# A decoder step's first tiles: order of first loads, rule for weight stores, staging buffers, single-token attention and the end of each attention

## The chip, the cores and the metric

The kernel runs on the 8 cores of one Trainium2 chip, as one program whose cores don't talk to each other. The metric is the device time of the slowest core in microseconds (us). Most executions agree within 0.3%; in some, the cores of one die run at a lower clock and the time is some per cent longer. Those slow runs are left out of every comparison here. Experiments ran on several chips, each beside the kernel before, so kernels of different calls are compared by their ratio to the kernel before.

## The reference, cut to what matters

One layer of a decoder, on 16 prompts of 2048 tokens and 32 single tokens with a cache:

```python
x = x + 0.5 * swiglu(rmsnorm(x, g1), w_gate1, w_up1, w_down1)      # FFN1, 1024 -> 2816 -> 1024
z = rmsnorm(x, g_mix) @ w_in       # pooling input | 3 head groups of q,k,v | gate_pool | gate_attn
# ... branch A: trailing means over 2, 4, 8, 16 tokens, a linear map for each group, -> w_pool_br
# ... branch B: window attention, (window, dilation) = (128,1), (512,4), (2048,16), rotary q and k,
#     the three outputs merged by their softmax denominators, -> w_attn_br
x = x + (sigmoid(gate_pool) * A + sigmoid(gate_attn) * B) @ w_o
x = x + 0.5 * swiglu(rmsnorm(x, g2), w_gate2, w_up2, w_down2)      # FFN2
# ... final rmsnorm; the rotated keys and the values are outputs too, in float32
```

All weights are float32 in memory; the kernel multiplies in bfloat16.

## The kernel before

Each core has 2 prompts and 4 single tokens (the "sample" rows). A prompt is 4 tiles of 512 tokens, so tiles 0 to 7. For each tile the program goes through a projection (q, k, v), an attention and a gate part, and fills TensorE's order there with matmuls of an FFN: FFN1's last third in tile 0, FFN2 of the tile before in the others. FFN1 of tiles 0 and 1 comes first and shares its weights. The single tokens ride along in the first tiles.

Weights stream in tiles of 512 KB bfloat16. The first use of a tile loads the float32 original, converted on the way, from GpSimd's queue (`w<-wt`). One of the uses then writes the bfloat16 copy to a scratch in memory (`wscr<-w`), and later uses load that copy from the Sync engine's queue (`w<-wscr`). `store_at` says which use writes it; until then each use is a float32 load.

```python
def store_at(tid):
    late = tid[0][:2] in ("gp", "ga", "wo") or tid[0] in ("wg1", "wu1", "wd1")
    return 1 if late and tid[1] % 2 else 0          # 0: first use stores, 1: second use
# ... w_issue: nth is how often this tile was loaded before
if nth <= at:
    pool.dma(slot[:, :], wt_d[ti, :, :], wsem[s][0], writes=slot.r)                    # float32, converted
else:
    sp.dma(slot[:, :], wscr[ti, :, :], wsem[s][2], reads=[scr_res[ti]], writes=slot.r) # bfloat16 copy
# ... wget, at the use itself
if first:
    sp.dma(wscr[ti, :, :], wsl[s][:, :], wsem[s][1], reads=wsl[s].r, writes=[scr_res[ti]])
```

In the projection a block of 128 tokens goes through small staging buffers, two each of `vst` (values), `kf` and `vf` (float32 keys and values), whose store is issued at once:

```python
sp.dma(v2scr[H.h, b * 128:(b + 1) * 128, :], vs[:, :], ds_vs.next(), reads=vs.r, writes=[v2res[H.h]])
v = vf.next()
dve.op(lambda: nc.vector.tensor_copy(out=v[:, :], in_=ps[bk][:, 256:512]), reads=[psr[bk]], writes=v.r)
sp.dma(kvp_d[2][s, r0:r0 + 128, 1, :], v[:, :], ds_vf.next(), reads=v.r)
# ... keys
rope_add(a_, b_, c0, c0 + 256, k_[:, :], k_.r)
sp.dma(dst, k_[:, :], ds_kf.next(), reads=k_.r)
```

The attention keeps up to three scored steps waiting for their product with V. At its end all three are consumed in one piece (`drain`), and `finish` scales the sums to `attnT`, which the gate part reads:

```python
def drain():
    while live:
        consume()      # two groups of PV matmuls, then perhaps a merge of `tot` on VectorE
    finish()
thunks.append(drain)
```

`K.later(t, f)` puts f off in the program's order by t us of TensorE work; `K.need(tag)` forces what was put off.

The softmax here doesn't subtract the row's maximum and nothing guards it: scores larger than these inputs give would overflow.

## Time and profile before

The median was 2959.34 us in the first four runs. The prediction shows the page's head, the stretches and the waits of the bad ones. More of TensorE's table of waits over the whole span of the kernel before (total us, times, longest us):

```profile
PE ps L590 <- DVE h L584: 36.8, 11, 22.7
...
PE ps L272 <- DVE tot L1248: 23.4, 26, 5.3
PE ps L272 <- DVE x L875: 13.2, 9, 2.8
```

`h` is the normalised block that TensorE transposes; its longest wait is the start of the kernel. `tot` are the merges of the attention: 26 waits for 23.4 us, spread over all tiles. In one quiet tile, the attention of tile 3 (1326 to 1412 us), they look like this:

```profile
PE ps L272 <- DVE tot L1248: 2.3, 4, 1.3
PE ps L272 <- DVE x L875: 1.1, 1, 1.1
```

VectorE updates `x` only after the merges.

### The profile page before, as it was taken

To read this page: it belongs to the slowest core of one execution; us is meant where nothing else is said; L and a number is where in the kernel's file an instruction comes from. 1 tells how busy PE (TensorE), PEld (TensorE's weight loads), DVE (VectorE), ACT (ScalarE), POOL (GpSimd) and SP (SyncE) were. 2 spreads that over 40 slices of the span, in tenths; PEclk is the share of its full clock that TensorE was granted. 3 is DMA by queue.
4 is the path that set the end of the run, shared out by engine and by line. 5 is a ranking of instruction groups with operands and counts; after the bars stand their busy time and mean duration, and the time that the engine had idled before them with its cause. 6 is when DMAs were issued, how large, how long until landed. Compare 5 with 4: busy or idle time off the path is not lost.

```text
span 2958.4 us, 48400 instructions; the slowest of 8 cores (2934.8 to 2958.4 us)
## 1 busy us (share of the span) xinstructions
PE 2789.3 (94%) x15833; PEld 1345.1 (45%) x15833; DVE 1302.1 (44%) x2055; ACT 915.9 (31%) x1949; POOL 443.6 (15%) x762
## 2 busy tenths in 40 slices
PE   6997878878999999999999999999999999999998
PEld 3443433434445544444444544454444444445443
DVE  2433644545334453345524454344633455254533
ACT  3102433324223342233413343143412433133321
POOL 2001011101003310041101401022100501023000
PEclk9998999999999999999999999999999999999999
DMA  9768578777547756563666456564565536455442
GB/s 216 157 129 197 144 146 203 164 162 205 190 143 196 194 191 208 184 208 115 227 202 196 141 189 207 183 202 132 185 208 185 182 125 214 154 161 172 158 155 100
DMA packets 153918, 519.84 MB, mean 176 GB/s; under 512 B 19619, under 2 KB 35787, under 8 KB 152711
## 3 DMA queue, kind: packets, MB, share of 16 engines
q1 hardware_dynamic: 136699, 457.18, 46.8%
q0 software_dynamic: 16976, 59.56, 13.1%
q8 instruction: 135, 2.21, 0.3%
q14 instruction: 108, 0.88, 0.1%
HBM read 496.95 MB, written 101.39 MB: 202 GB/s over the span
## 4 chain that ended last, share of the span: by engine, by line
PE 83%; DMA 8%; DVE 4%; issue 2%; ACT 2%; POOL 0%; DVEq 0%; SPq 0%; ACTq 0%; POOLq 0%
PE ps L272 80%; DMA w<-wt 2%; DMA s_kv<-c 2%; PE ps L282 2%; PE ps L590 1%; DVE tot L1248 1%; DMA w<-wscr 1%; DMA y<-x 1%; DMA gain<-gains 1%; DMA v2scr<-vst 1%; DVE h L584 0%; DMA wscr<-w 0%; DVE attnT L1261 0%; DVE x L875 0%; DVE x L584 0%
## 5 line engine op out<-in xcount | busy, mean ns | idle before, releaser
L272 PE MATMUL ps<-hT,w 128*128 128x512 bf16 x6912 | 1579.1, 382 | 30.7 <-DMA w<-wt 12.2
L272 PEld LDWEIGHTS ps<-hT,w 128*128 128x128 bf16 x6912 | 669.9, 98 | 814.4 <-issue 59.0
L272 PE MATMUL ps<-w,act 128*128 128x512 bf16 x2816 | 642.6, 382 | 26.4 <-DMA w<-wt 13.1
L864 DVE TENSOR_TENSOR act<-st,ps 128x512 bf16<-128x512 f32 x352 | 241.8, 687 | 573.7 <-PE ps L272 571.7
L272 PEld LDWEIGHTS ps<-w,act 128*128 128x128 bf16 x2816 | 270.9, 98 | 337.7 <-issue 41.9
L875 DVE SCALAR_TENSOR_TENSOR x<-ps,x 128x512 f32<-128x512 f32 x384 | 264.5, 691 | 257.8 <-PE ps L272 248.7
L853 ACT ACTIVATE st<-ps 128x512 f32<-128x512 f32 x190 | 113.4, 597 | 737.7 <-PE ps L272 728.0
L272 PE MATMUL ps<-w,hT 128*128 128x512 bf16 (+1 forms) x1280 | 277.8, 362 | 3.7 <-DMA w<-wt 2.1
L578 POOL TENSOR_SCALAR stat<-stat 128x1 f32<-128x1 f32 x128 | 43.5, 340 | 1536.4 <-ACT junk L575 1536.3
L575 ACT ACTIVATE junk<-x 128x1024 fp8e4<-128x1024 f32 x128 | 135.1, 1056 | 293.4 <-DVE x L875 185.2
L856 DVE SCALAR_TENSOR_TENSOR st<-st,ps 128x512 f32<-128x512 f32 x162 | 111.4, 688 | 247.1 <-ACT st L855 200.5
L272 PEld LDWEIGHTS ps<-w,hT 128*128 128x128 bf16 x1280 | 127.6, 102 | 126.6 <-issue 11.6
L855 ACT ACTIVATE st<-ps 128x512 f32<-128x512 f32 x162 | 96.7, 597 | 244.5 <-PE ps L272 241.5
L150 POOL DMA_DIRECT2D w<-wt x113 | 61.1, 542 | 628.6 <-PE ps L272 480.3
L584 DVE SCALAR_TENSOR_TENSOR h<-x,stat,gain 128x1024 bf16<-128x1024 f32 x96 | 122.6, 1279 | 40.0 <-DMA gain<-gains 20.0
L1218 ACT ACTIVATE P<-ps 128x512 bf16<-128x512 f32 (+1 forms) x160 | 90.2, 568 | 136.0 <-PE ps L272 115.5
L1013 ACT CAST qz<-ps 64x128 bf16<-64x128 f32 x384 | 99.7, 260 | 94.8 <-PE ps L282 68.1
L272 PE MATMUL ps<-w,mg 128*128 128x512 bf16 x512 | 115.7, 383 | 6.0 <-DMA w<-wt 3.8
L997 POOL TENSOR_TENSOR qkb<-tA,tB 128x256 bf16<-128x256 f32 (+1 forms) x140 | 85.2, 609 | 234.9 <-DVE tB L988 208.2
L594 ACT COPY hT<-ps 128x1024 bf16<-128x1024 bf16 x96 | 96.2, 1009 | 31.7 <-PE ps L590 31.3
L988 DVE TENSOR_TENSOR tA<-ps,rope 128x512 f32<-128x512 f32 x96 | 66.2, 690 | 79.0 <-PE ps L272 44.8
L590 PE MATMUL ps<-cbf,h 128*128 128x128 bf16 x768 | 61.3, 226 | 36.8 <-DVE h L584 36.8
(144 smaller groups left out, 1759.9 us busy)
## 6 DMA issues: line engine op xcount, KB each, us to landing
w<-wscr SPq DMA_DIRECT2D x602, 512.0 KB, 4.9
w<-wt POOLq DMA_DIRECT2D x113, 512.0 KB, 10.5
wscr<-w SPq DMA_DIRECT2D x92, 512.0 KB, 8.4
x<-x SPq DMA_DIRECT2D x32, 512.0 KB, 9.1
y<-x SPq DMA_DIRECT2D x32, 512.0 KB, 6.6
kvs<-c SPq DMA_DIRECT2D x32, 512.0 KB
gain<-gains SPq DMA_DIRECT2D x30, 512.0 KB, 8.1
kvp<-vf SPq DMA_DIRECT2D x42, 128.0 KB, 2.1
```

Of the source, the lines that this page charges most:

```text
L272: self.pe.op(lambda o=o, l=l, r=r, kw=kw: self.nc.tensor.matmul(o, l, r, **kw), reads=rds, writes=[self.psr[bank]] if i == 0 else (), inc= ...
L575: act.op(lambda: nc.scalar.activation(out=junk[0:n, :], in_=xap, func=AF.Square, scale=1.0 / 32, accum_out=st[:, 0:1], saturate=False), re ...
L584: dve.op(lambda: nc.vector.scalar_tensor_tensor(out=out, in0=xap, scalar=rs, in1=g[0:n, :], op0=ALU.mult, op1=ALU.mult), reads=xres + rr + ...
L590: pe.op(lambda c=c: nc.tensor.transpose(psb[b][:, c * n:(c + 1) * n], hb[0:n, c * 128:(c + 1) * 128], ident[0:n, 0:n]), reads=hb.r + cbf.r ...
L594: act.op(lambda: nc.scalar.copy(out=out, in_=psb[b][:, 0:8 * n].rearrange("p (c n) -> p c n", n=n)), reads=[psr[b]], writes=ores)
L853: act.op(lambda: nc.scalar.activation(out=st[:, :], in_=ps[bg][:, :], func=AF.Silu), reads=[psr[bg]], writes=st.r)
L855: act.op(lambda: nc.scalar.activation(out=st[:, :], in_=ps[bg][:, :], func=AF.Tanh, scale=0.5), reads=[psr[bg]], writes=st.r)
L856: dve.op(lambda: nc.vector.scalar_tensor_tensor(out=st[:, :], in0=st[:, :], scalar=1.0, in1=ps[bg][:, :], op0=ALU.add, op1=ALU.mult), read ...
L864: dve.op(lambda: nc.vector.tensor_tensor(out=ab[:, jl, :], in0=st[:, :], in1=ps[bu][:, :], op=ALU.mult), reads=st.r + [psr[bu]], writes=[a ...
L875: dve.op(lambda: nc.vector.scalar_tensor_tensor(out=xap, in0=ps[bk][:, :], scalar=scale, in1=xap, op0=ALU.mult, op1=ALU.add), reads=[psr[b ...
L1013: act.op(lambda: nc.scalar.copy(out=out, in_=in_), reads, writes)
L1218: act.op(lambda: nc.scalar.activation(out=P[:, 0:ncol], in_=ps[b][:, 0:ncol], func=AF.Exp, scale=0.125), reads=[psr[b]], writes=P.r)
```

## The change

Its intent is to win back TensorE's lost time in the first two tiles, without touching a matmul. It has seven parts:

1. Start: the norm's gain is loaded second instead of fifth, as 128 full rows instead of one repeated row; the first weights and tile 1's rows come later.
2. `store_at`: other uses write the bfloat16 copies. 92 stores remain, but float32 loads go from 113 to 169.
3. Four staging buffers of each kind instead of two (the new ones lie in `attnT` and `poolT`, which are idle then), and their stores are put off by 3 to 7 us, at most until the program asks for that buffer again.
4. Tile 0's rotary and pooling adds go from VectorE to GpSimd (`K.pass0`).
5. Sample attention: 7 of its 12 steps move from attention 1 into projection 1; exponentials and cache loads are put off further.
6. The drain is cut into three pieces with other matmuls between, and the scaling is put off 6 us.
7. Tile 1's projection starts with a head start: the first six entries of its list run before any FFN group (`run(fill[:6])`).

A few smaller delays moved as well (some norms, the reload of `v2scr`, the first sample loads), one bank list changed, and four dense groups at the end of the attention became three.

```diff
-        for b in range(4):
+        load_x(0, 0, sp)
+        load_gain(0, sp)
+        for b in range(1, 4):
             load_x(0, b, sp)
-        load_gain(0, sp)
 ...                                                   # (first weights later: cut)
         def store_at(tid):
-            late = tid[0][:2] in ("gp", "ga", "wo") or tid[0] in ("wg1", "wu1", "wd1")
-            return 1 if late and tid[1] % 2 else 0
+            nm, k = tid
+            if nm in ("wg1", "wu1", "wd1"):
+                return 1 + k % 2
+            if nm in ("wg0", "wu0", "wd0"):
+                return 1 if k < PARTS[0][1] else 0 if k < PARTS[1][1] else 1
+            return 1 if nm in ("ga", "wo") else 0
 ...
+        for n_ in range(2):
+            for rot, nm, at, res in ((vf, "vf", attnT.at, attnT.r), (kf, "kf", poolT.at, poolT.r)):
+                x_ = Buf(K, "%s%d" % (nm, 2 + n_), [128, 256], F32, at=at + 1024 * n_)
+                alias(x_.r, res)
+                rot.items.append(x_)
 ...                                                   # (vst likewise: cut)
-                                sp.dma(dst, k_[:, :], ds_kf.next(), reads=k_.r)
+                                K.later(7.0, lambda: sp.dma(dst, k_[:, :], ds_kf.next(), reads=k_.r), k_)
 ...                                                   # (values: 3.0 and 4.0, cut)
-            K.pass0 = i <= 1
+            K.pass0 = i == 1
 ...
+            if do_sample and i == 1:
+                sa = s_attend()
+                fill = [f for n in range(7) for f in fill[4 * n:4 * n + 4] + sa[n:n + 1]] + fill[28:]
+            if i == 1:
+                run(fill[:6])
+                fill = fill[6:]
 ...
             def drain():
-                while live:
+                if live:
                     consume()
-                finish()
-            thunks.append(drain)
+            thunks += [drain] * 3 + [finish]
 ...                                                   # finish:
+                K.later(6.0, scale, tag="attnT")
```

## The prediction

Its "section 3 of the page" is section 3 of the profile's page, the DMA queues, and not a page of the Trainium skill.

> **What bounds the kernel now.** I read the page's busy shares first, then the table of busy time by stretches, TensorE's table of waits, and the chain of waits for the bad stretches.
>
> ```profile
> span 2958.4 us, 48400 instructions; the slowest of 8 cores (2934.8 to 2958.4 us)
> PE 2789.3 (94%) x15833; PEld 1345.1 (45%) x15833; DVE 1302.1 (44%) x2055; ACT 915.9 (31%) x1949; POOL 443.6 (15%) x762
> ```
>
> TensorE is the bound: busy 94%, nothing else over half. The change neither adds nor removes a matmul (the order of the two programs has 15,829 each), so it can only win back TensorE's lost time. A busy share understates that loss, because slow matmuls count as busy. So I worked out a floor: in undisturbed stretches a 512-column matmul starts every 0.216 us (the chain of waits has one of 464 in 100.17 us); with the same kind of spacing for each other width (0.109 us at 256 columns, 0.055 at 128) the matmuls sum to 2,732 us. First matmul at 22.7 us, plus 2,732, plus 9 us from the last matmul to the end, leaves about 194 us lost between matmuls. The stretches say where:
>
> ```profile
> core 1: us, PE busy (x) PEld busy (x) DVE busy (x) ACT busy (x) POOL busy (x), PEclk, DMA share, GB/s
> 0.00:60.00 60.00, 32.80 (x204) 17.18 (x205) 15.37 (x26) 21.80 (x31) 16.90 (x33) 0.97 0.97 227
> 190.00:250.00 60.00, 50.35 (x423) 25.22 (x421) 19.33 (x26) 10.21 (x17) 6.99 (x15) 0.91 0.84 185
> 250.00:328.00 78.00, 61.94 (x332) 29.32 (x331) 44.84 (x98) 28.63 (x98) 8.00 (x14) 0.91 0.80 175
> 328.00:392.00 64.00, 48.18 (x360) 24.30 (x357) 38.55 (x89) 29.59 (x61) 3.10 (x7) 0.95 0.45 121
> 392.00:460.00 68.00, 56.14 (x258) 24.75 (x255) 25.64 (x36) 20.32 (x35) 11.86 (x23) 0.92 0.87 170
> 460.00:571.00 111.00, 95.65 (x484) 45.60 (x483) 57.11 (x111) 36.03 (x111) 10.80 (x21) 0.92 0.80 188
> 571.00:688.00 117.00, 93.29 (x528) 42.56 (x527) 58.44 (x112) 37.00 (x78) 9.33 (x19) 0.94 0.73 155
> 688.00:760.00 72.00, 63.64 (x515) 32.03 (x514) 34.40 (x58) 25.67 (x48) 12.05 (x24) 0.96 0.85 234
> 760.00:1064.00 304.00, 298.45 (x2057) 150.98 (x2054) 125.05 (x200) 90.97 (x203) 56.33 (x90) 0.99 0.61 173
> 1064.00:2825.00 1761.00, 1738.88 (x9281) 835.49 (x9278) 793.22 (x1180) 579.24 (x1209) 295.01 (x491) 1.00 0.55 181
> ```
>
> I cut these stretches at the stage boundaries of the program. Seven of them, 190 to 760 us (tiles 0 and 1, where the weights come for the first time), are 570 us long and hold 432 us of floor: 138 us lost. The DMA engines' share there is 0.80 or more in five and the granted clock is 0.91 to 0.96. From 1064 us on the loss is 1%. What TensorE waits for in 190 to 760:
>
> ```profile
> PE ps L272 <- DMA w<-wt: 31.1, 12, 8.1
> PE ps L272 <- ACT s_P L771: 12.5, 3, 6.0
> PE ps L272 <- DVE tot L1248: 11.7, 7, 5.3
> PE ps L282 <- DVE qkb L997: 8.4, 1, 8.4
> ```
>
> The columns are total us, times and longest us. First come float32 weights, then the single-token group's softmax, then merges of attention sums, then a rotary result. The chain of waits in 249 to 345 shows what lies behind the last one:
>
> ```profile
> 252.32 10.47 DMA w<-wt
> 265.25 11.79 DMA v2scr<-vst
> 277.10 5.70 DMA v2scr<-vst
> ...
> 314.62 5.73 DMA kvp<-kf
> ```
>
> A staging buffer (two each of vst, kf, vf) is refilled only when its store has landed, 6 to 12 us in a busy queue; ScalarE waits for that, VectorE for ScalarE, TensorE for VectorE.
>
> **What the Trainium skill says.** "TensorE: Matmul & The Clock Gate", part 1 on the HAM clock gate: an idle window of about 3.4 us halves TensorE's clock. The trace agrees: the clock record has half-rate stretches in multiples of 3.4 us after each long wait, 10.2 us of them from 225.9 and from 280.5. In 190 to 760 they sum to 78 us; the loss of 138 us is about 108 of gaps over 0.45 us and 30 of slow matmuls and smaller gaps. So a removed long gap is worth about 1.25 times its length. "DMA: Bandwidth & Descriptors", section "Queues, rings and completion order": each DMA engine takes turns between queue rows, and the section on issuing engines says all issuers run on the same 16. The trace agrees: in the first 60 us loads of x took 17.1 us from the Sync queue and weights 12.7 us from the GpSimd queue, both slow. "GPSIMD Engine Reference", section 3: two-input elementwise work is about twice as slow there as on VectorE; here a rotary add of 128x256 takes 724 ns against 425.
>
> **The change, part by part.** DMA work first. Section 3 of the page gives two rates at a full share: the GpSimd queue holds 13.1% of 2958 us, 388 us, for 113 weight loads that each read 1.05 MB of float32 (118.5 MB), so 0.306 MB/us; the Sync queue 457 MB in 46.8%, 0.33 MB/us.
>
> Start. Before, the first norm waits for gain, which was issued behind four x loads and beside two weights, and lands at 21.1 us. Now gain is second in the queue, and is read as 128 full rows. I expect it at 7 us. But the weights are issued only after the first block's statistics (9 us instead of 2.3), and the Sync queue has no scratch store in it that waits, so all of tile 1's x and the second gain are in flight beside them: two weights, 2.1 MB at half the rate, land near 24 us. TensorE's first FFN matmul moves from 28.7 to about 24.5: -4. The 5.9 us lost in the first FFN stage fall to 4 (tile 1's transposes now stand between other matmuls): -2.
>
> Stores of converted weights move. Stage by stage I counted loads and stores from the two programs' issue order, in MB moved, with the floor in us:
> 190 to 250, tile 0's last third of FFN1 alone: 12.6 float32, 6.3 stores, 2.1 bfloat16 before; 16.8 float32 only after. At the rates 67 us against 55, floor 47. Loss 12.2 to 3.5: -9.
> 250 to 460 (projection, attention, gate of tile 0): 43.7 MB before, 52.5 after, 139 against 167 us for a floor of 153 us. Part of the DMA gain is handed back here.
> 460 to 760 (all of tile 1): 76.9 before, 74.7 after, but with 51.3 instead of 38.8 through the slower queue: 242 against 239 us, floor 232. No relief in sum.
> 760 to 1122 (FFN1, projection, attention and gate of tile 2): 70.2 before, 85.9 after, 268 us of DMA work beside a floor of 349: room enough.
>
> So DMA stays near the bound up to 760 us, and the gains must come from waits.
> Projection 0 (loss 21.6): four staging buffers instead of two, stores issued 3 to 7 us later so that they do not block the Sync queue, rotary adds on GpSimd. The two chains above (8.4 and 3.5 us of gaps, 13.7 us of half clock) go; new waits on weights and GpSimd come: to 13, -9.
> Attention 0 (19.8): its 9 us of waits on tot shrink, since the drain is cut into three with matmuls between, and the pooling adds leave VectorE: to 11, -9. Gate 0 (16.1): fewer stores: -5.
> Projection 1 (23.3): starts with six projection groups, so the 4.9 us wait for normalised rows is covered: -9, after the sample steps that move in here.
> Attention 1 (33.4): twelve cache loads of 10 to 19 us each against two buffers and a step every 7 us; seven steps move to the projection, where a step comes every 13 us: to 15, -18. Gate 1 (11.7): more float32 weights, fewer waits: 0.
> 760 to 1122: float32 loads rise from 15 to 33 in projection and attention 2, all through GpSimd in front of its rotary adds: +4.
> Tiles 3 to 7: each attention loses about 4.7 us, of which 1.6 is the drain (merges and two PV groups back to back) and 1.1 the x update behind the merges; with the cut drain and the deferred scaling about 2.7 go, five times 2.4 after small costs, less 2 for tile 3's float32 loads: -10.
> Sum: -4 -2 -9 -9 -9 -5 -9 -18 +0 +4 -10 = -71 us, so 2959 - 71 = 2888.
>
> **Rivals.** First, DMA takes over: stores moved, not removed, and 56 more float32 loads (29 MB more read). For it: shares of 0.80 to 0.87, and 406 us of DMA work from 250 to 760 against a floor of 385. If tiles 0 and 1 run at the DMA rate with the imbalance of today, only the start, 190 to 250, the sample steps and the drains pay, about 38 us: 2920. Against: the shares are below one because of blocked queues, which the deferred stores mend.
> Second, GpSimd in tile 0: loads wait there in order for free slots, and now the rotary adds stand behind them. For it: GpSimd waited 253 us for TensorE and 35 us for scratch stores in 190 to 760. Each such wait of 5 us behind a projection would go to TensorE: +15, 2903. Against: it has 15% to do, and the adds of a block are issued ahead of the loads that its last use frees.
> Third, better than I think: the long gaps vanish together with their half clocks, leaving 40 us of loss in 190 to 760 instead of my 79: about 2850.
>
> **Range and chances.** 2% of 2959 is 59 us, so the line is at 2900, 12 us above my figure. The terms -9 and -18 could each be off by half, mostly together, since all depend on the DMA queue: a range from 2855 to 2925. Chance of faster by over 2%: 0.64; within 2%: 0.34; slower: 0.02, since no stage gets new work on TensorE.
>
> **What would show it.** Right: first FFN matmul at 23 to 26 us; the wait on DVE qkb around 287 gone; ACT s_P waits below 4 us in all; waits on DVE tot below 10 us over the span (26 waits and 23.4 us before); the half-clock stretches halved; DMA share above 0.85 from 250 to 460. Wrong: TensorE waiting for POOL qkb by over 10 us (second rival), for w from either source by over 45 us (first), or tiles 2 and 3 losing over 10 us more than now.

## More of the kernel before

From the page, the GpSimd queue, the memory traffic and the issues of float32 weight loads (here: count, KB, us to landing):

```profile
q0 software_dynamic: 16976, 59.56, 13.1%
HBM read 496.95 MB, written 101.39 MB: 202 GB/s over the span
...
w<-wt POOLq DMA_DIRECT2D x113, 512.0 KB, 10.5
```

## The result, and the profile after

The changed kernel has a median of 2878.38 us in 10 runs (2875.01 to 3262.83, two of them slow). Its ratio to the kernel before is 0.9723, with a 95% interval of 0.9711 to 0.9736. Ratios here are the mean time of one kernel's fast runs over that of the other's fast runs of the same rounds, so not quite the ratio of the medians. It is faster by 2.8%; the prediction said 2888 us.

The page of the changed kernel, with the lines that answer to those of before:

```profile
span 2877.6 us, 48549 instructions; the slowest of 8 cores (2860.9 to 2877.6 us)
PE 2772.8 (96%) x15833; PEld 1342.5 (47%) x15833; DVE 1285.3 (45%) x2017; ACT 913.6 (32%) x1949; POOL 526.7 (18%) x892
...
q0 software_dynamic: 25040, 88.93, 19.5%
...
HBM read 526.31 MB, written 101.39 MB: 218 GB/s over the span
...
w<-wt POOLq DMA_DIRECT2D x169, 512.0 KB, 10.7
```

The count of matmuls is unchanged. The memory reads rose by 29 MB and the GpSimd queue's share by half, yet a float32 load still lands in 10.7 us in the median (10.5 before). GpSimd took on 83 us of work.

The stretches at the changed kernel's own stage boundaries (core 5, its slowest; columns as in the prediction's table). In order: FFN1's last third; projection, attention, gate of tile 0; the same of tile 1; FFN1, projection and attention of tile 2; the rest:

```profile
core 5: us, PE busy (x) PEld busy (x) DVE busy (x) ACT busy (x) POOL busy (x), PEclk, DMA share, GB/s
0.00:60.00 60.00, 38.69 (x234) 19.29 (x235) 17.10 (x29) 22.70 (x33) 16.45 (x33) 1.00 0.92 182
184.00:234.00 50.00, 47.42 (x404) 24.51 (x401) 19.20 (x26) 10.43 (x18) 8.56 (x18) 1.00 0.90 159
234.00:307.00 73.00, 61.33 (x326) 28.84 (x324) 31.27 (x57) 27.77 (x95) 33.87 (x59) 0.93 0.85 177
307.00:366.00 59.00, 47.71 (x352) 24.01 (x350) 30.75 (x59) 29.47 (x63) 29.66 (x46) 0.97 0.97 225
366.00:434.00 68.00, 56.91 (x269) 25.69 (x267) 28.12 (x39) 21.28 (x36) 10.95 (x22) 0.92 0.79 155
434.00:538.00 104.00, 94.65 (x496) 45.54 (x494) 64.82 (x131) 40.03 (x126) 11.97 (x22) 0.97 0.78 167
538.00:627.00 89.00, 85.68 (x519) 41.40 (x518) 49.56 (x91) 30.52 (x61) 8.88 (x18) 0.98 0.70 136
627.00:702.00 75.00, 63.13 (x519) 32.08 (x518) 36.94 (x62) 27.94 (x51) 16.98 (x32) 0.91 0.99 230
702.00:1000.00 298.00, 296.44 (x2052) 150.10 (x2050) 121.34 (x200) 89.79 (x202) 66.04 (x109) 1.00 0.80 200
1000.00:2744.00 1744.00, 1736.64 (x9277) 835.86 (x9274) 797.56 (x1204) 578.56 (x1212) 310.08 (x508) 1.00 0.58 187
```

Compare stretch by stretch with the table in the prediction. FFN1's last third took 60 us and takes 50; attention 1 took 117 and takes 89. Gate 1, with 75 where it had 72, now has the lowest clock (0.91) and the fullest DMA (0.99) of the table. And in the 298 us of tile 2 the DMA share rose from 0.61 to 0.80 while TensorE's busy share rose from 98.2% to 99.5%: the extra transfers cost nothing there.

A busy share hides slow matmuls, so I compared losses: for each stage the time from matmul start to matmul start, less 0.216, 0.109 or 0.055 us by width (0.025 to 0.029 for the narrowest), the spacing of the prediction's floor. A wait of 2.4 us lies right at the boundary of projection 1 and attention 1 of the changed kernel; the table gives it to attention 1. On the slowest core of each profile:

| stage | lost before | lost after | change | predicted |
|---|---|---|---|---|
| first FFN matmul, at | 28.7 | 22.4 | -6.3 | -4 |
| first FFN stage | 5.9 | 5.7 | -0.2 | -2 |
| FFN1, last third, tile 0 | 12.2 | 2.8 | -9.4 | -9 |
| projection 0 | 21.6 | 17.3 | -4.3 | -9 |
| attention 0 | 19.8 | 14.8 | -5.0 | -9 |
| gate 0 | 16.1 | 15.5 | -0.6 | -5 |
| projection 1 | 23.3 | 14.5 | -8.8 | -9 |
| attention 1 | 33.4 | 6.4 | -27.0 | -18 |
| gate 1 | 11.7 | 15.0 | +3.3 | 0 |
| tile 2 | 13.8 | 8.1 | -5.7 | +4 |
| tiles 3 to 7 | 25.4 | 8.3 | -17.1 | -10 |
| last | 7.1 | 7.4 | +0.3 | 0 |
| sum | | | -80.8 | -71 |

TensorE's waits over the whole span of the changed kernel:

```profile
PE ps L272 <- DMA w<-wt: 38.1, 9, 11.7
PE ps L612 <- DVE h L606: 24.0, 8, 11.7
PE ps L272 <- ACT hT L616: 5.6, 4, 1.9
PE ps L272 <- DVE tot L1279: 4.0, 9, 1.6
PE ps L272 <- ACT tot L1036: 2.7, 4, 1.3
PE ps L282 <- POOL qkb L1020: 2.6, 1, 2.6
...
PE ps L272 <- ACT s_P L793: 1.9, 2, 0.9
```

`tot` went from 23.4 us to 4.0, `s_P` from 12.5 to 1.9, the rotary wait from 8.4 to 2.6, the waits for normalised blocks fell by 13 us. Waits for float32 weights rose from 31.1 to 38.1. So the kernel's largest remaining wait is the one that the change fed. Together with those for bfloat16 copies (8.2 us before, 1.7 after) the waits for weights hardly changed, though: 39.3 us before, 39.8 after. In tile 3's attention (1262 to 1344 us of the changed kernel) one line is left of the two:

```profile
PE ps L272 <- DVE tot L1279: 0.3, 1, 0.3
```

In projection 0 the chain of waits still goes through memory (start us, us, what):

```profile
236.91 14.60 DMA w<-wt
251.64 1.88 PE ps L272 x4
254.81 10.30 DMA v2scr<-vst
265.20 7.16 DMA v2scr<-vst
...
273.74 5.48 DMA wscr<-w
```

Four staging buffers instead of two, and still two `v2scr` landings stand in the chain. I took this for a leftover worth mending and tested it (the ninth run).

### The profile page after: what moved, and what is told of

It is laid out like the page before. It is cut to its first block, busy times and chain, and to the rows that moved or that the text cites. A ratio compares the mean times of both kernels' runs of the same rounds, so it can differ in the third digit from the quotient of the medians.

```text
span 2877.6 us, 48549 instructions; the slowest of 8 cores (2860.9 to 2877.6 us)
## 1 busy us (share of the span) xinstructions
PE 2772.8 (96%) x15833; PEld 1342.5 (47%) x15833; DVE 1285.3 (45%) x2017; ACT 913.6 (32%) x1949; POOL 526.7 (18%) x892
## 3 DMA queue, kind: packets, MB, share of 16 engines
q1 hardware_dynamic: 128635, 427.81, 44.6%
q0 software_dynamic: 25040, 88.93, 19.5%
## 4 chain that ended last, share of the span: by engine, by line
PE 89%; DMA 5%; DVE 2%; issue 1%; ACT 1%; POOL 1%; SPq 0%; DVEq 0%; POOLq 0%; ACTq 0%
PE ps L272 86%; DMA w<-wt 3%; PE ps L282 2%; PE ps L612 1%; DMA v2scr<-vst 1%; DMA wscr<-w 1%; DVE tot L1279 1%; DMA x<-x 0%; DMA w<-wscr 0%; ACT junk L597 0%; DVE h L606 0%; POOL qkb L1020 0%; ACT P L1249 0%; DVE x L898 0%; POOL w L150 0%
## 5 line engine op out<-in xcount | busy, mean ns | idle before, releaser
L272 PE MATMUL ps<-w,act 128*128 128x512 bf16 x2816 | 635.3, 379 | 9.4 <-DMA w<-wt 9.4
L272 PEld LDWEIGHTS ps<-w,act 128*128 128x128 bf16 x2816 | 270.3, 98 | 314.5 <-issue 14.4
L150 POOL DMA_DIRECT2D w<-wt x169 | 92.0, 546 | 695.6 <-PE ps L272 614.5
L1020 POOL TENSOR_TENSOR qkb<-tA,tB 128x256 bf16<-128x256 f32 (+1 forms) x164 | 100.4, 612 | 220.4 <-DVE tB L1011 193.6
L616 ACT COPY hT<-ps 128x1024 bf16<-128x1024 bf16 x96 | 96.3, 1010 | 25.8 <-PE ps L612 25.4
L601 POOL TENSOR_TENSOR stat<-stat,mhalf 128x1 f32<-128x1 f32 x128 | 95.3, 745 | 19.6 <-POOL stat L600 1.2
## 6 DMA issues: line engine op xcount, KB each, us to landing
w<-wt POOLq DMA_DIRECT2D x169, 512.0 KB, 10.7
```

The source lines that it names most:

```text
L272: self.pe.op(lambda o=o, l=l, r=r, kw=kw: self.nc.tensor.matmul(o, l, r, **kw), reads=rds, writes=[self.psr[bank]] if i == 0 else (), inc= ...
L601: pool.op(lambda: nc.gpsimd.tensor_tensor(out=st[:, 2:3], in0=st[:, 1:2], in1=mhalf[0:n, :], op=ALU.pow), reads=r + mhalf.r, writes=r)
L616: act.op(lambda: nc.scalar.copy(out=out, in_=psb[b][:, 0:8 * n].rearrange("p (c n) -> p c n", n=n)), reads=[psr[b]], writes=ores)
L1020: e.op(lambda h=h, op=op: ne.tensor_tensor(out=ov[:, :, h, :], in0=av[:, :, h, :], in1=bv[:, :, 1 - h, :], op=op), reads=a_.r + b_.r, writ ...
```

## The experiments

Twelve kernels ran, and each gave the reference's results. My theory after the result: the drain is the largest part, since it acts in every tile; staging and sample steps pay in tiles 0 and 1; the store rule only moves loss between stages of tile 0. Its rivals: the store rule pays as the prediction had it, or the deferral of the stores matters and not the number of buffers.

"Cost" below is the ratio to the kernel before, less 0.9723, times 2958 us: what undoing that part costs. With the intervals of both ratios taken as independent, a cost is good to about 8 us. One caution goes with it: the kernel before averaged 2953 to 2954 us in the experiments and 2959 beside the changed kernel, so costs lean on that scaling; without it each would be up to 6 us smaller. Costs under 8 us are therefore called unresolved, and those of 10 and 12 us are barely resolved.

Losses by stage, mean of the six cores whose traces hold all matmul records (cores 0 and 6, in the tenth run cores 2 and 4, lack about 300 of 15,833), one profile each. Two profiles of kernels with the same projection 1 can differ there by 4 us, so a single small difference in this table shows nothing.

| stage | before | changed | e1 stores | e2 staging | e3 sample | e4 drain | e10 |
|---|---|---|---|---|---|---|---|
| FFN1, last third, tile 0 | 11.1 | 2.1 | 10.0 | 1.6 | 1.4 | 0.8 | 1.3 |
| projection 0 | 21.1 | 15.0 | 8.3 | 28.0 | 15.0 | 14.9 | 12.7 |
| attention 0 | 21.0 | 15.3 | 7.5 | 13.7 | 14.4 | 22.0 | 10.2 |
| gate 0 | 15.9 | 14.6 | 11.8 | 13.9 | 14.2 | 12.3 | 13.8 |
| projection 1 | 19.5 | 10.9 | 12.3 | 15.8 | 8.6 | 7.8 | 8.4 |
| attention 1 | 30.6 | 5.4 | 10.8 | 5.7 | 13.3 | 9.9 | 5.4 |
| gate 1 | 9.6 | 13.7 | 7.1 | 15.0 | 14.1 | 13.8 | 8.4 |
| attention 2 | 6.3 | 1.2 | 1.3 | 1.2 | 1.2 | 7.3 | 1.2 |
| tiles 3 to 7 | 25.4 | 8.7 | 8.6 | 14.0 | 9.5 | 25.4 | 8.7 |
| half-clock time | 93.3 | 48.9 | 43.2 | 70.5 | 53.5 | 59.7 | 38.7 |

### The old rule for the stores

```diff
-            (the new store_at)
+            late = tid[0][:2] in ("gp", "ga", "wo") or tid[0] in ("wg1", "wu1", "wd1")
+            return 1 if late and tid[1] % 2 else 0
```

> The changed kernel with the old rule for which use of a weight tile writes its bfloat16 copy to scratch. Theory (waits, not bytes): the new rule pays only where tile 0's last third of FFN1 runs alone (loss 12.2 us before, 2.8 after), so undoing it costs 8 to 14 us: about 2889 us, ratio to before 0.976, and the loss in that stage comes back to 10 us or more while the later stages of tile 1 stay as in the changed kernel. Rival (the DMA schedule carries the whole gain in tiles 0 and 1): undoing it costs 25 us or more: 2905 us or above.

Median 2881.28 us, ratio 0.9743 (0.9719 to 0.9767): a cost of 6 us, unresolved. The stages moved much more than the time. FFN1's last third loses 7.9 us again and attention 1 another 5.4, but projection 0, attention 0, gate 0 and gate 1 together lose 24 us less than in the changed kernel. TensorE's waits in this run, on its slowest core:

```profile
PE ps L272 <- DMA w<-wt: 30.3, 12, 8.0
...
PE ps L272 <- DMA w<-wscr: 10.0, 2, 7.4
```

Both sources together come to 40.3 us, where the changed kernel has 39.8 (38.1 and 1.7). The rule changes where TensorE waits for weights, not how long. Over the stages of the table this one profile of the old rule even loses 9 us less. So it is not shown that the new rule pays at all.

### The old staging: two buffers, stores at once

```diff
-        (the four new buffers of vf and kf, the two of vst)
-                                K.later(7.0, lambda: sp.dma(dst, k_[:, :], ...), k_)
+                                sp.dma(dst, k_[:, :], ...)                  # and the four others
```

> The changed kernel with two staging buffers each of vst, kf, vf again and with their stores issued at once. Theory of the prediction: staging made projection 0 lose its two chains, so undoing it costs 8 to 12 us, all in projection 0 and 1: about 2888 us. Rival, from the changed kernel's chain of waits (v2scr stores still land one behind another, 10.3 and 7.2 us, each waiting for the one before because they are all marked as writing one scratch region): the buffers buy little, 0 to 4 us: 2878 to 2882.

Median 2903.38 us, ratio 0.9824 (0.9796 to 0.9853): a cost of 30 us. That is beyond the 8 to 12 us expected. Projection 0 loses 13 us more, projection 1 5 more, projection 2 2.3 more, and tile 3 5.3 more. The last two had not been counted by the prediction at all.

### The old sample attention

```diff
-                fill = [f for n in range(7) for f in fill[4 * n:4 * n + 4] + sa[n:n + 1]] + fill[28:]
-                K.later(8.0, lambda: s_cache(n + 2), ...)     # and the exponential at once; head start kept
+                K.later(2.5, lambda: s_cache(n + 2), ...)
+                (all 12 steps in attention 1, one after each step there)
```

> The changed kernel with all twelve steps of the single-token attention in tile 1's attention stage again, with the old delays. Theory: the sample steps cost attention 1 most of its 33 us, so undoing them costs 15 to 22 us: about 2897 us, with attention 1's loss back above 22 us. Rival: attention 1 got better because fewer scratch stores and loads compete there (26.2 MB before, 17.0 after): undoing the sample steps costs under 8 us.

Two of four runs were fast (2885.45 and 2885.66 us), ratio 0.9765 (0.9736 to 0.9793): a cost of 12 us (8 without the scaling), below the 15 to 22 expected. Attention 1 loses 7.9 us more and projection 1, without the steps, 2.3 less. TensorE's wait for the sample's softmax:

```profile
PE ps L272 <- ACT s_P L793: 5.3, 4, 1.6
```

5.3 us, not the 12.5 of the kernel before, though the steps sit where they sat. The same steps hurt less in company of the other parts, perhaps because the cache loads now share the queues with fewer waiting stores in attention 1 (17 MB of DMA issued there instead of 26, by the two programs' orders). That last reason is argued from the orders, not isolated.

### The old drain

```diff
-                if live:
+                while live:
                     consume()
-            thunks += [drain] * 3 + [finish]      # and the scaling 6 us later, three dense groups left behind it
+                finish()                          # and the scaling at once
+            thunks.append(drain)                  # four dense groups
```

> The changed kernel with the drain in one piece, the scaling of attnT at once and four dense groups behind it. Theory: it carries the gain of tiles 3 to 7 (attention loses 4.6 us before, 1.4 after), so undoing it costs about 3.2 us in each of six attention stages and a little in tiles 0 and 1: 18 to 24 us, about 2898 us. Rival: the loss went with the deferred stores and less VectorE work: under 6 us.

Median 2911.11 us, ratio 0.9848 (0.9826 to 0.9871): a cost of 37 us (33 without the scaling), the largest of all parts undone whole, and well above the 18 to 24 expected. TensorE's waits in that run:

```profile
PE ps L272 <- DVE tot L1279: 21.2, 25, 3.0
PE ps L272 <- DVE x L898: 14.5, 8, 3.6
```

Both lines of the kernel before are back at their size (23.4 and 13.2). By stage: attention 0 +6.7, attention 1 +4.5, attention 2 +6.1, and 16.7 over tiles 3 to 7, some 3.3 each; together 34 us. The six-core mean of the span rose by less, 26 us, because projection 1 and gate 0 lost 5 us less in this one profile.

### The old order of the first loads

```diff
-        load_x(0, 0, sp); load_gain(0, sp); ...          # then the other x blocks
+        for b in range(4):
+            load_x(0, b, sp)
+        load_gain(0, sp)                                  # still as 128 full rows
+        w_issue(2); for b in range(4): load_x(1, b, sp)
```

> The changed kernel with the old order of the first loads (four x blocks, then gain, two weights issued at once, tile 1's x at once); gain still read as 128 full rows. Theory: the order brings the whole 7 us by which the first FFN matmul moved (29.3 to 22.2 us as the mean of the cores), so undoing it costs 6 to 8 us and that matmul is back at 28 to 30 us. Rival of the prediction (weights issued late take back half): 2 to 4 us. If reading gain as full rows were the cause instead, the first FFN matmul would stay below 25 us.

Median 2882.99 us, ratio 0.9756 (0.9734 to 0.9778): a cost of 10 us (4 without the scaling). The first FFN matmul is back at 28.4 us (six-core mean; 22.2 changed, 29.3 before). VectorE's wait for the gain, then TensorE's for the normalised blocks:

```profile
DVE h L609 <- DMA gain<-gains: 19.6, 1, 19.6
```

```profile
PE ps L615 <- DVE h L609: 30.8, 8, 22.4
```

The gain was read here as full rows and still came after 19.6 us. So the full rows alone bring nothing; it is the order of the loads that pays. Whether their form helps in the new order no run tested. The first matmul's own delay is 6.2 us.

### Two buffers with the stores still put off, and four with the stores at once

```diff
-        (the new buffers)                        # e6_two_buffers: only this
```
```diff
-  K.later(7.0, lambda: sp.dma(dst, k_[:, :], ...), k_)
+  sp.dma(dst, k_[:, :], ...)                     # e7_stores_at_once: only this, all five stores
```

> The changed kernel with two buffers each of vst, kf, vf, stores still deferred by 3 to 7 us. Half of what the old staging did together (+25 us as the mean of the cores, 13 in projection 0, 5 in projection 1, 2 and 5 in projections 2 and 3). If the number of buffers is what counted (the theory of the prediction), this costs 15 us or more, most in projection 0. If the Sync queue blocked by stores that wait was what counted, this costs under 8 us. A third way: buffers alone are worse than both undone (over 25 us), since a deferred store then holds its buffer longer.

> The changed kernel with four buffers, but each staging store issued at once. If the number of buffers is what counted: under 8 us lost. If the blocked Sync queue is what counted: 15 us or more, with projection 0's loss above 22 us and bfloat16 weights late in projections 2 and 3.

These two split the staging part, and they came out as neither theory alone had it, but as the third way named beforehand (over 25 us for two buffers). Four buffers with stores at once: 2879.02 us, ratio 0.9745 (0.9723 to 0.9768), a cost of 7 us, unresolved; the mean span of its eight cores is even 2 us below the changed kernel's. Two buffers with stores put off: 2916.78 us, ratio 0.9875 (0.9856 to 0.9894), a cost of 45 us, 15 more than with both undone. Both ran on the same chip, three and four fast runs, each set within 2.4 us: 38 us apart. TensorE's waits in the run with two buffers, over the whole span:

```profile
PE ps L282 <- POOL qkb L1128: 15.8, 8, 3.3
...
PE ps L282 <- DVE tB L1000: 8.2, 1, 8.2
```

The second of these lies in projection 0, and it is not what the deferral added: with both undone that stage loses as much (28.0 us, here 27.0). The 15 us lie in tiles 3 to 7, which lose 28.8 us here and 14.0 with both undone (six-core means). There (1150 to 2700 us) GpSimd makes the rotary keys and waits for the stores of its buffers, and TensorE waits for GpSimd:

```profile
POOL kf L1009 <- DMA kvp<-kf: 22.3, 8, 3.7
```

```profile
PE ps L282 <- POOL qkb L1128: 11.9, 6, 2.6
```

With both undone, TensorE has no such wait in these tiles. A store that is put off holds its buffer longer; when the program asks for that buffer again, the store is issued at last, and the writer waits until it has landed. With four buffers that is hidden. The deferral by itself earned nothing that shows. What counts is the number of buffers.

### Tile 0's rotary adds on VectorE again

```diff
-            K.pass0 = i == 1
+            K.pass0 = i <= 1
```

> The changed kernel with tile 0's rotary and pooling adds on VectorE again instead of GpSimd. Theory of the prediction: the move helps tile 0's attention (VectorE 31 us busy there instead of 39) more than it costs in waits on GpSimd (qkb 4.6 us, pT 2.4 us): undoing it costs 3 to 10 us, in attention 0. The prediction's second rival: GpSimd holds tile 0 up, and undoing it gains 3 to 8 us in projection 0.

Two of four runs were fast (2879.93 and 2878.30 us). By stage attention 0 loses 5 us more, and projections 0 and 1 5 us less in sum. The run with the stores at once has fast runs of 2877.48 to 2879.52 us and is itself not told apart from the changed kernel. So no effect of this part shows; with two fast runs that is inconclusive rather than zero.

### A record of landing for each block of values

The kernel keeps one record of who last wrote the `v2scr` scratch, so each block's store waits for the landing of the one before. The chain above shows two such landings.

```diff
-        v2res = [Res("v2scr%d" % i) for i in range(2)]
+        v2res = [[Res("v2scr%d_%d" % (i, j)) for j in range(4)] for i in range(2)]
-                                ... writes=[v2res[H.h]])
+                                ... writes=[v2res[H.h][b]])
```

> The changed kernel, with the scratch region of the residue-ordered values marked as written per 128-row block instead of as a whole, so that a block's store no longer waits for the landing of the block before. Theory: these landings (10.3 and 7.2 us in the chain of projection 0) are the wait that is left of the staging problem; removing them takes 4 to 9 us, to about 2870 us, from projection 0 and 1. Rival: the DMA queues are the bound there and the next wait (weights, single-token stores) takes its place: 0 to 2 us.

Median 2875.32 us, ratio 0.9723 (0.9708 to 0.9738): no difference to the changed kernel, to within about 6 us by the two intervals. The chain of waits in projection 0 of this run:

```profile
236.26 13.14 DMA w<-wt
249.53 16.82 PE ps L272 x68
...
303.57 5.31 DMA kvs<-s_kst
```

The two landings are gone from the chain, and TensorE works 16.8 us through. But it had not stood there in the changed kernel either. That kernel's TensorE during the two landings (columns as in the stretches):

```profile
252.00:273.00 21.00, 21.00 (x97) 8.84 (x96) 8.34 (x15) 7.67 (x29) 6.54 (x10) 0.94 0.95 196
```

It was busy for all of the 21 us, with other matmuls. I had read the chain without looking whether TensorE was idle beside it. Projection 0 lost 12.5 us instead of 15.0, which is less than the scatter of one profile, and attention 0 and gate 0 lost 1.1 more: the float32 load ahead of the chain stands as it was, and a store of the single-token group now stands in it further on. A long link in a chain of waits is worth only its lead over the next one, and nothing where the engine that bounds the kernel has other work meanwhile.

### A third rule for the stores

If the rule only moves waits for weights, the stores should go where there is room: the 0.80 of tile 2's stretch instead of gate 1's 0.99. On top of the last edit:

```diff
             if nm in ("wg0", "wu0", "wd0"):
-                return 1 if k < PARTS[0][1] else 0 if k < PARTS[1][1] else 1
-            return 1 if nm in ("ga", "wo") else 0
+                return 1 if k == 0 else 0 if k < PARTS[1][1] else 2      # last third: third use
+            return 2 if nm in ("gp", "ga", "wo") and k % 2 else 0        # odd ones: third use
```

> As e9, and with a third rule for the scratch stores: FFN1's last third stored only at its third use (tile 2, where DMA has room), gate and output weights half at the first and half at the third use, FFN1's first two thirds at the first use but for the very first tiles. It keeps the DMA work of 184 to 234 us as in the changed kernel and takes 6.3 MB from tile 0's projection and attention and 8.4 MB from tile 1's gate. If DMA work per stage sets the loss there, 8 to 18 us faster than e9: about 2858 us. If not (the new rule and the old one differ by 6 us), within 4 us of e9.

Median 2861.58 us, ratio 0.9686 (0.9672 to 0.9701). Against the last kernel (mean of fast runs 2860.8 against 2872.9) it is 12 us faster. Stretches of this run (core 7, its slowest) at the same times as the changed kernel's above; gate 0, gate 1 and tile 2:

```profile
366.00:434.00 68.00, 62.57 (x317) 29.28 (x317) 33.27 (x51) 22.63 (x47) 11.29 (x20) 0.95 0.89 195
...
627.00:702.00 75.00, 72.67 (x557) 37.49 (x558) 34.13 (x61) 28.27 (x48) 13.38 (x22) 1.00 0.78 213
702.00:1000.00 298.00, 296.44 (x2042) 149.38 (x2041) 127.75 (x207) 91.10 (x205) 73.42 (x125) 1.00 0.90 207
```

The stages come earlier in this run, by 6 us at gate 0 and 17 at gate 1, so these are the same times rather than exactly the same work. From 627 to 702 us there are 72.67 us of matmuls where the changed kernel had 63.13; the DMA share fell from 0.99 to 0.78. Tile 2's share rose to 0.90 and its matmuls stayed at 296.44. By stage gate 1 loses 5 us less and attention 0 also 5 less, while tile 2's gate, from 977 us on, loses 3 more, in a wait for normalised blocks (6.0 us on core 7, 2.8 in the changed kernel); why, no run shows. And TensorE's wait for float32 weights over the span fell from 38.1 us to

```profile
PE ps L272 <- DMA w<-wt: 20.6, 8, 6.2
```

```diff
-                return 1 if k == 0 else 0 if k < PARTS[1][1] else 2
+                return 1 if k == 0 else 0 if k < PARTS[1][1] else 2 if k < 9 else 0
```

> As e10, but of FFN1's last third only half waits for the third use and half is stored at the first use: 3.1 MB more in 184 to 234 us, 3.2 MB less in tile 0's projection and attention, 6.3 MB less in tile 2's FFN1. If loss grows faster than in proportion to DMA work beyond a stage's floor, spreading wins: 2 to 6 us faster than e10; if each MB costs the same anywhere, equal to e10 within 2 us.

Half of the last third's stores went back to the first use: 2871.14 us, ratio 0.9719 (0.9704 to 0.9734), 10 us slower than the run above, against an expected gain of 2 to 6. FFN1's last third loses 9.5 us again instead of 1.3. From 184 to 234 us the DMA share is 0.98 with these stores and 0.78 without. That stage has no room for them, and some 10 of the 12 us above hang on this one choice.

### Without the head start of projection 1

```diff
-            if i == 1:
-                run(fill[:6])
-                fill = fill[6:]
```

> The changed kernel without the six projection pieces that tile 1 runs ahead of the first woven FFN group. Theory of the prediction: they cover the wait for tile 0's normalised rows (4.9 us of waits of TensorE on VectorE's h before, plus 10 us at half clock), so without them projection 1 loses 6 to 9 us more: about 2883 us. Rival: projection 1 got better through fewer scratch stores and more staging buffers (the old staging cost 5 us there), and the head start is worth under 3 us.

Median 2880.18 us, ratio 0.9748 (0.9729 to 0.9767): a cost of 7 us, unresolved (fast runs 2877.39 to 2882.35). Projection 1, where the prediction put the gain, loses only 0.5 us more; attention 1 loses 3.3 more. With the wait at their boundary given to projection 1 it is 2.0 and 1.7.

## Why the prediction was right, point by point

The time was 10 us below the predicted one and inside the range. The frame held: TensorE's lost time was the only thing to win, and none of the time came from anywhere else. The terms were less good than their sum: tile 0 and gate 1 fell 16 us short, attention 1, tile 2 and tiles 3 to 7 brought 26 more than predicted. That these largely cancel is luck.

**The start (-4; -6.3 measured).** Right in kind, wrong in what limits it: I expected the weights to land last, near 24 us. From 0 to 75 us TensorE waited 18.0 us for normalised blocks and never for a weight. The prediction cites turn-taking between queues for this term and says that the trace agrees; that loads from both queues were slow fits it, but does not show it.

**FFN1's last third (-9; -9.4).** Right, and the store rule is the cause: with the old rule the loss returns (10.0 us).

**Projection, attention and gate of tile 0 (-23 in sum; -9.9).** The step that failed is "part of the DMA gain is handed back here", after which I took no loss for it. More than all of it was handed back: with the old rule these three stages lose 17 us less than in the changed kernel, and FFN1's last third only 7.9 more. So the store rule loses in tile 0, as the first rival had it for this part. The gain in projection 0 came from staging (13 us by the second run), more than my -9, and the store rule took about half of it (6.7). In attention 0 the old drain costs 6.7 us and rotary adds on VectorE 5 (one profile each); the store rule takes 7.8 back.

**Projection 1 (-9; -8.8).** The right number by a wrong way. I credited the head start, as six groups where it has four; without it projection 1 lost 0.5 to 2 us more. The staging buffers gave 4.9 us here. With the boundary's wait counted here the change is -5.9 and not -8.8.

**Attention 1 (-18; -27.0).** All of it was put down to the sample steps. The third run gives them 7.9 us of stage and 12 of time; the old stores cost 5.4 here, the old drain 4.5 and the missing head start 3.3. These four add to 21 of the 25 us of the six-core mean. Where the remaining 4 come from stays open.

**Gate 1 (0; +3.3).** "More float32 weights, fewer waits" was wrong in its second half: 11.7 us of its loss is a single wait for a float32 weight, and with the rule of the tenth run the stage loses 8.4 us instead of 13.7 (six-core mean).

**Tile 2 (+4; -5.7) and tile 3.** The extra float32 loads cost nothing that shows: projection 2 lost 1.3 us before and after. But staging is part of why: with the old staging projection 2 and tile 3 lose 2.3 and 5.3 us more. I had also forgotten the drain in attention 2, worth 6.1.

**Tiles 3 to 7 (-10; -17.1).** This term was 7 us too small. I found the two waits and subtracted "small costs" from a gain of 2.7 us per tile. There were no such costs, and the gain is 3.3 to 3.4 per tile; the fourth run takes 3.3 of it back. That the part beyond 2.7 is an after-effect of the waits, such as slow matmuls, was not isolated. Over all attentions the drain is worth 33 to 37 us, some two fifths of the whole change, and I had most of it unnamed in other stages.

**Staging.** I named both the buffers and a Sync queue unblocked by deferred stores. The deferral gave nothing that shows; the buffers did.

The checks named beforehand: the first FFN matmul came at 22.4, just before my 23 to 26. The rotary wait of 8.4 us is gone. `s_P` is below 4 us and `tot` below 10. Half-clock time fell from 93 to 49 us in the six-core mean. The DMA share from 234 to 434 us is 0.87, from the three stretches weighted by their length. None of the signs of a wrong prediction showed: GpSimd's rotary results held TensorE for 4.6 us, weights from both sources for 39.8 (the limit was 45, but the kernel before had 39.3, so this sign could hardly tell).

Undone one at a time, the parts cost about 6 (stores), 30 (staging), 12 (sample), 37 (drain), 10 (start) and 7 (head start): some 102 us against 82 measured (0.0277 of 2958). From the plain means of the fast runs, without the scaling, the six sum to 74. So whether they overlap can't be told, and the small ones may be nothing.

## What to carry to other kernels

A wait of 2 us that comes back in every tile is worth more than a wait of 8 us in one: before mending the bad stretch, multiply the harmless lines by the number of times they run, and leave other matmuls between a last group of products and what reads them. When stores of a streaming conversion have to go somewhere, count the DMA share of each stage and put them where it is low, two or three uses later if need be: a rule that only moves them inside the full stages earns nothing. Deferring a store keeps its buffer busy longer, so add the buffers first. And before mending a link in a chain of waits, look whether the engine that bounds the kernel is idle during it.

## What the Trainium skill lacked or had wrong

- "DMA: Bandwidth & Descriptors", section "SWDGE vs HWDGE vs iDMA": it says that a DMA that converts must come from GpSimd, but not what it costs. Here the time goes by the bytes read: 177.2 MB of float32 in 169 loads took 19.5% of 2877.6 us, 0.316 MB/us at a full share, against 427.8 MB in 44.6%, 0.333 MB/us, for the Sync queue. By these two rates a converting load of a 512 KB tile takes 2.1 times as long as a plain one (estimate: 1.05 MB at 0.316 against 0.52 MB at 0.333).
- "TensorE: Matmul & The Clock Gate", section "HAM oscillation": it sizes the cost of a throttled stretch as half of its length. From 190 to 760 us of the kernel before that would be 39 us for 78 us of half clock; slow matmuls and all gaps under 0.45 us came to 30 us, since 27.5 of the 78 us fall into the gaps over 0.45 us, where no matmul runs that could be slowed.
- No page I looked at weighs a store that is put off, which holds its buffer longer, against the queue that it leaves free: with two buffers the kernel took 2916.78 us deferred and 2903.38 us not (ratios 0.9875 and 0.9824); with four buffers there was no difference that the runs resolve.
